# The down projection of a hybrid decoder layer by seven block products in place of eight

## The chip, the cores and the metric

The kernel runs on one core of one Trainium2 chip. The metric is the device time of one execution in microseconds (us). Below, PE is TensorE (matmul), PEld its weight load, DVE is VectorE, ACT is ScalarE, POOL is GpSimd and SP is SyncE, on which most DMA transfers are issued; ACT issues the others.

## The reference

One decoder layer on 512 tokens of 1024 channels: a mixer (matrix-memory heads beside a convolution group) and then a ConvFFN, each between two normalisations and with a residual. The change is in the ConvFFN's last part:

```python
u = rms_norm(x, ffn_pre_g[l]) * (1.0 + sc2) + sh2
up = causal_dwconv(u @ ffn_up[l], ffn_conv_w[l], ffn_conv_b[l])   # 1024 -> 2 x 2816, 3 taps
a, gt = jnp.split(up, 2, axis=-1)
f = (jax.nn.silu(gt) * a) @ ffn_down[l]                           # 512 x 2816 times 2816 x 1024
x = x + g2 * rms_norm(f, ffn_post_g[l])
```

## The kernel before

**Products.** Operands are float32. Each is split into a high part (rounded to the matmul's fp32r format) and a low part (the rest); a product of two operands is three matmuls, high by high, high by low and low by high (`mm3`, lines 186 to 190), all added into one PSUM bank. A matmul has a stationary block of 128 x 128 and a moving one of 128 x 512.

**Splitting weights.** `w_load` loads a row block of 128 x 2048 into one of two `raw` buffers from SP's queue; `w_split` makes the high part of each quarter on ACT (line 170) and the low part on POOL (line 171), into the pool `w` of 20 buffers.

**Up projection.** The loop over i = 0 to 21 (line 920 on) makes block i of `a` and of the gate on PE, does the three-tap convolution (ACT line 915, DVE line 917), the silu (ACT) and the product (DVE line 945), and splits the result into `fh` and `fl` (lines 951, 952), which lie with the contraction on the partitions and the 512 tokens along the row. They are kept in the pool of 44 `slot` buffers. `u2h` and `u2l` are the input's parts, in the pool `upool`.

**Down projection.** The result is four token tiles (tt) of 128 by two column halves (hf) of 512, one PSUM bank each: eight banks, all there are. For each of the 22 row blocks k of the weights every bank takes one `mm3`, tokens of `fh`/`fl` stationary and 512 weight columns moving: 22 x 4 x 2 x 3 = 528 matmuls. The first 18 row blocks go over all token tiles; the last four are done token tile after token tile (line 979), 24 matmuls each.

**The end.** For each token tile SP loads two residual tiles `xr` (line 985); DVE multiplies each bank by the gain row `g2r` (line 988), ACT takes the sum of squares, DVE and POOL make the token's factor (lines 615, 617), DVE adds the residual (line 993), and SP stores the result (line 994).

**Order.** PE and SP run their instructions in the order of the program text. On DVE, ACT and POOL a scheduler orders them when the program is built. Every engine then works its list strictly from the top, and each instruction waits there for what it needs: data, a buffer, or a transfer.

Of the kernel before, what the change touches and what calls it, by code (L numbers as in the profile page):

```python
# [14 lines left out]
ALU = mybir.AluOpType  # L15
# [37 lines left out]
def decoder_layer(ctx, tc, w_glu0, x, c, adaT, vecs, w_glu, w_qko, w_v0, w_v, w_out, w_up, w_down, out):  # L53
# [30 lines left out]
    def slot(name, dt=F32):  # L84
        return slots.tile([P, T], dt, tag="t", name=name)
# [4 lines left out]
    def atbank(name):  # L90
        return psum.tile([P, T], F32, tag="at", bufs=2, name=name)
# [528 lines left out]
    def tok(tt):  # L620
        return slice(tt * P, (tt + 1) * P)
# [298 lines left out]
    f = []  # L920
    for i in range(NF):
# [23 lines left out]
        V.tensor_tensor(out=a, in0=a, in1=g, op=ALU.mult)  # L945
# [5 lines left out]
        S.activation(hi, a, AF.Copy)  # L951
        V.tensor_tensor(out=lo, in0=a, in1=hi.bitcast(F32), op=ALU.subtract)
        f.append((hi, lo))


    KD = 18
    fsq = const.tile([P, 2 * NT], F32, name="fsq")
    banks = [[atbank(f"dn{tt}_{hf}") if tt == 0 else cvbank(f"dn{tt}_{hf}") if tt == 1 else mmbank(f"dn{tt}_{hf}")
              for hf in range(2)] for tt in range(NT)]
    wd = {}  # L960

    def down_rows(k):

        if k % 2 == 0:
            pieces = w_load(w_down[k // 2], f"wd{k}")
            wd[k], wd[k + 1] = pieces[:2], pieces[2:]
        return wd[k]

    def down_mm(k, tt):
        for hf in range(2):  # L970
            mm3(banks[tt][hf], (f[k][0][:, tok(tt)], f[k][1][:, tok(tt)]), wd[k][hf], k == 0, k == NF - 1)

    for k in range(KD):
        down_rows(k)
        for tt in range(NT):
            down_mm(k, tt)
    for k in range(KD, NF):
        down_rows(k)
    for tt in range(NT):
        for k in range(KD, NF):  # L980
            down_mm(k, tt)
# [4 lines left out]
        for hf in range(2):  # L986
            m = slot(f"fo{tt}_{hf}")
            V.tensor_tensor(out=m, in0=banks[tt][hf], in1=g2r[hf], op=ALU.mult)  # L988
            sq_sum(banks[tt][hf], fsq[:, 2 * tt + hf : 2 * tt + hf + 1], f"dn{tt}_{hf}")
            res.append(m)  # L990
# [6 lines left out]
def _layout(i):  # L997
# [9 lines left out]
    def tiles(w, starts, per):  # L1007
# [34 lines left out]
        "w_down": c_(f("ffn_down")[0].reshape(NF // 2, 2, P, D).transpose(0, 2, 1, 3).reshape(NF // 2, P, 2 * D)),  # L1042
# [19 lines left out]
```

## Time and profile before

| | us |
|---|---|
| median of 3 runs (797.0 to 800.23) | 797.66 |
| span of the profiled execution, first to last instruction | 794.8 |
| up projection's last matmul starts | 667.59 |
| down projection's first and last matmul start | 667.83, 787.44 |
| last store is issued (the second of two from 791.06) | 791.7 |

The page does not give the profiled execution's own time, only its span. A view of windows gives for each engine the busy time in a stretch, then the clock that TensorE was granted (1.00 is full), the share of the 16 DMA engines and the rate in GB/s. A row of the timeline has the start, the time, the engine, the line and what it writes and reads; "x2" joins two instructions in a row, so that the time shown for both is less than twice the mean where the second starts before the first has ended. In brackets is the engine's idle time before it and what ended that. The last number of a DMA row is the time from issue to landing.

### The profile page before, as it was taken

Reading aid. Unit: us, or ns where it says so; the run is one execution under the profiler, and the core shown is the slowest. Engines: PE = TensorE matmul, PEld = TensorE weight load, DVE = VectorE, ACT = ScalarE, POOL = GpSimd, SP = SyncE. Lnnn points to the kernel's source line nnn. Section 1 sums busy time; section 2 is a strip of 40 time slices with the busy share of each in tenths; the row PEclk is TensorE's granted clock in tenths of the full one; section 3 lists DMA queues with packets and bytes.
Section 4 is the critical chain, followed back from the end, with each engine's and each line's share of the span. In section 5 each row is a group of like instructions: output and inputs, shape, how many; then the busy total and the mean of one; then the engine's idle time right before and its main releaser. Section 6 shows DMA issues by size and latency. Waiting matters only on the chain.

```text
span 794.8 us, 10281 instructions
## 1 busy us (share of the span) xinstructions
PE 776.3 (98%) x3749; PEld 647.8 (81%) x3749; DVE 470.1 (59%) x737; ACT 378.5 (48%) x707; POOL 436.3 (55%) x357
## 2 busy tenths in 40 slices
PE   7899999899999999999999999999999999999996
PEld 4678898678888888888889988888888888888885
DVE  7659999999997334537968794454444453000014
ACT  6576428668574555561345454444444444222212
POOL 3689749769788443442941474444454444454420
PEclk9999999999999999999999999999999999999998
DMA  8973313313126331426854653322332222323205
GB/s 294 328 290 110 108 54 106 132 33 131 52 92 216 117 133 54 160 106 233 323 186 159 215 183 106 107 71 89 106 107 106 100 93 99 106 107 106 79 1 185
DMA packets 24886, 106.95 MB, mean 135 GB/s; under 512 B 2914, under 2 KB 2946, under 8 KB 17412
## 3 DMA queue, kind: packets, MB, share of 16 engines
q1 hardware_dynamic: 16740, 83.22, 29.9%
q10 hardware_dynamic: 8096, 23.08, 8.3%
q8 instruction: 29, 0.48, 0.3%
q14 instruction: 21, 0.17, 0.1%
HBM read 102.08 MB, written 4.21 MB: 134 GB/s over the span
## 4 chain that ended last, share of the span: by engine, by line
PE 73%; DVE 15%; DMA 4%; ACT 3%; issue 2%; POOL 1%; DVEq 0%; POOLq 0%; SPq 0%; ACTq 0%
PE up L189 10%; PE up L190 10%; PE up L188 10%; DVE cv L661 7%; PE dn L190 5%; PE dn L189 5%; PE dn L188 5%; PE glu L189 2%; PE glu L190 2%; PE glu L188 2%; DMA wglu<-in_w_glu 2%; PE mixa L190 2%; PE mixa L188 2%; PE mixa L189 2%; PE mixb L190 2%; PE mixb L189 2%
## 5 line engine op out<-in xcount | busy, mean ns | idle before, releaser
L661 DVE SCALAR_TENSOR_TENSOR cv<-gt,cvw,cv 128x506 f32<-128x506 f32 (+24 forms) x200 | 134.2, 728 | 0.4
L988 DVE TENSOR_TENSOR fo<-dn,g2r 128x512 f32<-128x512 f32 x8 | 5.5, 692 | 100.1 <-PE dn L190 100.1
L171 POOL TENSOR_TENSOR wup_1024l<-wup,wup_1024h 128x512 fp32r<-128x512 f32 x20 | 26.9, 1345 | 31.9 <-ACT wup_1024h L170 22.4
L171 POOL TENSOR_TENSOR wup_1536l<-wup,wup_1536h 128x512 fp32r<-128x512 f32 x20 | 27.1, 1355 | 29.1 <-ACT wup_1536h L170 29.0
L657 POOL TENSOR_TENSOR cs<-cs,cs 128x510 f32<-128x510 f32 (+3 forms) x32 | 41.8, 1305 | 0.2
L171 POOL TENSOR_TENSOR wup_512l<-wup,wup_512h 128x512 fp32r<-128x512 f32 x20 | 26.8, 1338 | 23.1 <-ACT wup_512h L170 23.1
L171 POOL TENSOR_TENSOR wup_0l<-wup,wup_0h 128x512 fp32r<-128x512 f32 x20 | 27.0, 1349 | 21.1 <-ACT wup_0h L170 21.1
L189 PE MATMUL up<-u2l,wup_0h 128*128 128x512 f32 (+1 forms) x100 | 36.5, 365 | 0.2 <-DVE u2l L830 0.2
L188 PE MATMUL up<-u2h,wup_0h 128*128 128x512 f32 (+1 forms) x100 | 36.5, 365 | 0.0
L188 PE MATMUL up<-u2h,wup_1024h 128*128 128x512 f32 (+1 forms) x100 | 36.5, 365 | 0.0
L190 PE MATMUL up<-u2h,wup_0l 128*128 128x512 f32 (+1 forms) x100 | 36.4, 364 | 0.0
L188 PE MATMUL up<-u2h,wup_1536h 128*128 128x512 f32 (+1 forms) x100 | 36.4, 364 | 0.0
L189 PE MATMUL up<-u2l,wup_1536h 128*128 128x512 f32 (+1 forms) x100 | 36.4, 364 | 0.0
L188 PE MATMUL up<-u2h,wup_512h 128*128 128x512 f32 (+1 forms) x100 | 36.4, 364 | 0.0
L190 PE MATMUL up<-u2h,wup_1536l 128*128 128x512 f32 (+1 forms) x100 | 36.4, 364 | 0.0
L189 PE MATMUL up<-u2l,wup_512h 128*128 128x512 f32 (+1 forms) x100 | 36.4, 364 | 0.0
L190 PE MATMUL up<-u2h,wup_512l 128*128 128x512 f32 (+1 forms) x100 | 36.4, 364 | 0.0
L190 PE MATMUL up<-u2h,wup_1024l 128*128 128x512 f32 (+1 forms) x100 | 36.4, 364 | 0.0
L189 PE MATMUL up<-u2l,wup_1024h 128*128 128x512 f32 (+1 forms) x100 | 36.4, 364 | 0.0
L155 DVE SCALAR_TENSOR_TENSOR junk<-ada,cb 128x1024 bf16<-128x1024 f32 x20 | 31.5, 1576 | 6.2 <-DMA ada<-in_adaT 6.0
L171 POOL TENSOR_TENSOR wd_1024l<-wd,wd_1024h 128x512 fp32r<-128x512 f32 x11 | 14.2, 1293 | 29.4 <-ACT wd_1024h L170 29.4
L171 POOL TENSOR_TENSOR wd_0l<-wd,wd_0h 128x512 fp32r<-128x512 f32 x11 | 14.3, 1296 | 28.0 <-ACT wd_0h L170 28.0
(723 smaller groups left out, 2613.5 us busy)
## 6 DMA issues: line engine op xcount, KB each, us to landing
wup<-in_w_up SPq DMA_DIRECT2D x22, 1024.0 KB, 4.8
wqko<-in_w_qko SPq DMA_DIRECT2D x12, 1024.0 KB, 4.8
wd<-in_w_down SPq DMA_DIRECT2D x11, 1024.0 KB, 4.8
ada<-in_adaT ACTq DMA_DIRECT2D x20, 512.0 KB, 5.6
ada<-in_adaT SPq DMA_DIRECT2D x16, 512.0 KB, 6.7
wo<-in_w_out SPq DMA_DIRECT2D x8, 1024.0 KB, 4.8
spare<-in_adaT ACTq DMA_DIRECT2D x12, 512.0 KB, 8.3
wglu<-in_w_glu SPq DMA_DIRECT2D x5, 1024.0 KB, 7.8
```

Source lines behind the costliest of these rows:

```text
L155: t = V.scalar_tensor_tensor(out=junk, in0=r, scalar=1.0, in1=cb, op0=ALU.mult, op1=ALU.mult, accum_out=mod[:, i : i + 1])
L171: (eng or G).tensor_tensor(out=lo[:, :n], in0=src, in1=hi[:, :n].bitcast(F32), op=ALU.subtract)
L188: PE.matmul(ps, a[0], b[0], start=start, stop=False)
L189: PE.matmul(ps, a[0], b[1], start=False, stop=False)
L190: PE.matmul(ps, a[1], b[0], start=False, stop=stop)
L657: G.tensor_tensor(out=side[:, d:], in0=side[:, d:], in1=t[:, d:], op=ALU.add)
L661: last_tap = V.scalar_tensor_tensor(out=cp[:, d:], in0=cvx[j][:, : T - d], scalar=w(CK - 1 - d), in1=cp[:, d:], op0=ALU.mult, op1=ALU.add)
L988: V.tensor_tensor(out=m, in0=banks[tt][hf], in1=g2r[hf], op=ALU.mult)
```

## The change

The contraction of 2816 is taken as eleven row blocks m of 2 x 128. In each, the activations are a 2 x 2 block matrix (two halves of 256 tokens by two halves of the contraction: a11, a12, a21, a22), and the weights too (b11 to b22, 128 x 512 each). Strassen's scheme in Winograd's form needs seven products of such blocks in place of eight. A product of one block is two token tiles q of 128, each with a bank of its own: 7 x 11 x 2 x 3 = 462 matmuls of the same shape.

Since seven products of two banks are 14 and there are eight banks, there are two phases. Phase one makes p1, p5, p6 and p7 over all m; phase two p2, p3 and p4. Between them the four sums are taken out of PSUM and added.

- In the up projection `forms` makes the combinations s1 to s4 of a pair of blocks on DVE (256 columns each), splits a11, s3, s1 and s2, and stores a12, a22 and s4 to DRAM (`g2_d`) from ACT's queue.
- In phase one `load1` loads three quarters of a weight row block, and `forms1` makes t1, t2 and t3 by three subtractions on DVE and splits four pieces. The high parts are ACT's as before, the low parts DVE's (function `split`); POOL has no part in it. t2 is stored to DRAM. There are two more raw buffers (`more`, in the place of `u2h`).
- In phase two `load2` loads two quarters and t2, `forms2` makes t4 and splits three pieces, `load_g2` loads the stored activations and `forms_g2` splits them.
- The end takes the token tiles in the order p2 and p3 for tiles 0 and 1, then p4 alone for tiles 2 and 3, whose other halves are complete after phase one. The last two row blocks (m = 9, 10) are done product after product in both phases.

The low parts of a weight row block of 2 x 128 before, on POOL (wd8 is the raw block, h and l are high and low parts; the last row is the next block's first):

```order
L171 TENSOR_TENSOR wd8_0l_6404<-wd8_6401,wd8_0h_6403 128x512
L171 TENSOR_TENSOR wd8_512l_6408<-wd8_6401,wd8_512h_6407 128x512
L171 TENSOR_TENSOR wd8_1024l_6412<-wd8_6401,wd8_1024h_6411 128x512
L171 TENSOR_TENSOR wd8_1536l_6416<-wd8_6401,wd8_1536h_6415 128x512
L171 TENSOR_TENSOR wd10_0l_6470<-wd10_6467,wd10_0h_6469 128x512
```

The same place now, on DVE in phase one (b, t and wd name weights; L1012 to L1014 are the subtractions, L927 the low parts):

```order
L1013 TENSOR_TENSOR wd1_5_6358<-wd1_5_6358 128x512
L927 TENSOR_TENSOR t2_4l_6447<-wd1_4_6311,t2_4h_6446 128x512
L927 TENSOR_TENSOR b1_5l_6481<-wd1_5_6358,b1_5h_6480 128x512
L1012 TENSOR_TENSOR wdmore_6238<-wdmore_6238 128x512
L1014 TENSOR_TENSOR wd1_5_6358<-wd1_5_6358 128x512
L927 TENSOR_TENSOR t1_5l_6485<-wd1_5_6358,t1_5h_6484 128x512
L927 TENSOR_TENSOR t3_5l_6489<-wd1_5_6358,t3_5h_6488 128x512
```

Four operations of POOL for each row block became seven of DVE; the subtractions of the next row block stand among the low parts of this one.

At the change of phase, on ACT, now (nothing corresponds to it before): g2h0 is the high part of the first stored activations, s40 that of their s4; t4_2h and b2_3h are weights of row blocks 2 and 3.

```order
L926 ACTIVATE t4_2h_6889<-wd2_13_6705 128x512
L926 ACTIVATE b2_3h_6924<-wdmore_6238 128x512
L926 ACTIVATE g2h0_6789<-g2kept_6239 128x512
L926 ACTIVATE s40_6791<-g2kept_6239 128x256
L926 ACTIVATE g2h1_6831<-g2kept_6239 128x512
```

And on DVE, where g2l0 is the low part, and su, s3 and sp5 are sums out of PSUM:

```order
L927 TENSOR_TENSOR t4_2l_6890<-wd2_13_6705,t4_2h_6889 128x512
L1085 TENSOR_TENSOR s3_0_6769<-p7_0_6236,su_0_6753 128x512
L1085 TENSOR_TENSOR s3_1_6770<-p7_1_6237,su_1_6754 128x512
L927 TENSOR_TENSOR b2_3l_6925<-wdmore_6238,b2_3h_6924 128x512
L1087 TENSOR_TENSOR su_0_6753<-su_0_6753,sp5_0_6737 128x512
L927 TENSOR_TENSOR g2l0_6790<-g2kept_6239,g2h0_6789 128x512
L1087 TENSOR_TENSOR su_1_6754<-su_1_6754,sp5_1_6738 128x512
L927 TENSOR_TENSOR s40_6791<-g2kept_6239,s40_6791 128x256
```

The first activations of phase two are split behind weights of its second and third row block, though the text asks for them first.

At the end on DVE, before: L988 is the product with g2r, L993 the residual addition.

```order
L988 TENSOR_TENSOR fo2_0_6883<-dn2_0_6133,g2r_5897 128x512
L988 TENSOR_TENSOR fo2_1_6887<-dn2_1_6134,g2r_5897 128x512
L615 TENSOR_SCALAR ro2t_6891<-fsq_6128 128x1
L993 SCALAR_TENSOR_TENSOR fo2_0_6883<-fo2_0_6883,ro2r_6893,xr2_0_6879 128x512
L993 SCALAR_TENSOR_TENSOR fo2_1_6887<-fo2_1_6887,ro2r_6893,xr2_1_6881 128x512
```

At the end on DVE, now: L1127 is the addition out of PSUM, L1130 the product with g2r, L1134 the residual addition.

```order
L1127 TENSOR_TENSOR su_1_6754<-p3_1_6780,su_1_6754 128x512
L1134 SCALAR_TENSOR_TENSOR fo0_0_7224<-fo0_0_7224,ro0r_7233,xr0_0_7217 128x512
L1134 SCALAR_TENSOR_TENSOR fo0_1_7229<-fo0_1_7229,ro0r_7233,xr0_1_7219 128x512
L1130 TENSOR_TENSOR fo1_1_7263<-su_1_6754,g2r_5981 128x512
L1127 TENSOR_TENSOR s3_0_6769<-p4_0_6781,s3_0_6769 128x512
L615 TENSOR_SCALAR ro1t_7265<-fsq_6229 128x1
L1127 TENSOR_TENSOR s3_1_6770<-p4_1_6782,s3_1_6770 128x512
L1130 TENSOR_TENSOR fo2_0_7286<-s3_0_6769,g2r_5981 128x512
L615 TENSOR_SCALAR ro2t_7288<-fsq_6229 128x1
L1130 TENSOR_TENSOR fo3_0_7309<-s3_1_6770,g2r_5981 128x512
L615 TENSOR_SCALAR ro3t_7311<-fsq_6229 128x1
L1134 SCALAR_TENSOR_TENSOR fo1_0_7258<-fo1_0_7258,ro1r_7267,xr1_0_7251 128x512
```

Before, the operations of one token tile stand together; now the second tile's residual additions stand behind the sums of tiles two and three. SP's order is the same as before: the two stores of a tile, then the two xr of the next.

The diff, cut:

```diff
--- before.py
+++ after.py
@@ -917,7 +917,33 @@
             V.scalar_tensor_tensor(out=t[:, d:], in0=ps[:, : T - d], scalar=w(2 - d), in1=t[:, d:], op0=ALU.mult, op1=ALU.add)
         return t
 
-    f = []
+    NM = NF // 2
+    g2_d = [dram.tile([P, 3 * HT], F32, tag=f"g2d{m}", name=f"g2d{m}") for m in range(NM)]
+    t2_d = [dram.tile([P, T], F32, tag=f"t2d{m}", name=f"t2d{m}") for m in range(NM)]
+    pairs = []
+
+    def split(src, hi, lo):
+        S.activation(hi, src, AF.Copy)
+        V.tensor_tensor(out=lo, in0=src, in1=hi.bitcast(F32), op=ALU.subtract)
+
+    def forms(m, F):
+
+        a11, a21, a12, a22 = (F[:, b * HT : (b + 1) * HT] for b in range(4))
+        s1, s2 = ysum[:, :HT], ysum[:, HT:]
+        s4 = ysq[:, (m % 2) * HT : (m % 2 + 1) * HT]
+        V.tensor_tensor(out=s1, in0=a21, in1=a22, op=ALU.add)
+        V.tensor_tensor(out=a21, in0=a11, in1=a21, op=ALU.subtract)
+        V.tensor_tensor(out=s2, in0=s1, in1=a11, op=ALU.subtract)
+        V.tensor_tensor(out=s4, in0=a12, in1=s2, op=ALU.subtract)
+        own = []
+        for n, z in enumerate((F[:, :T], ysum)):
+            hi, lo = slot(f"fh{m}_{n}", F32R), slot(f"fl{m}_{n}", F32R)
+            split(z, hi, lo)
+            own.append((hi, lo))
+        pairs.append(own)
+        nc.scalar.dma_start(g2_d[m][:, :T], F[:, T : 2 * T])
+        nc.scalar.dma_start(g2_d[m][:, T:], s4)
+
     for i in range(NF):
...
         a = conv3(pa, i, f"fa{i}")
         g = conv3(pg, NF + i, f"fg{i}")
         S.activation(g, g, AF.Silu)
-        V.tensor_tensor(out=a, in0=a, in1=g, op=ALU.mult)
-        if i < 2:
-            hl = vpool.tile([P, 2 * T + 8], F32R, tag="vh", name=f"fhl{i}")
-            hi, lo = hl[:, :T], hl[:, T : 2 * T]
+        if i % 2 == 0:
+            F = vpool.tile([P, 2 * T + 8], F32, tag="vh", name=f"F{i // 2}")
+        V.tensor_tensor(out=F[:, (i % 2) * T : (i % 2 + 1) * T], in0=a, in1=g, op=ALU.mult)
+        if i % 2:
+            forms(i // 2, F)
+
+
+    M1 = NM - 2
+    M2 = NM - 2
+    fsq = const.tile([P, 2 * NT], F32, name="fsq")
+    p1 = [atbank(f"p1_{q}") for q in range(2)]
+    p5 = [cvbank(f"p5_{q}") for q in range(2)]
+    p6 = [mmbank(f"p6_{q}") for q in range(2)]
+    p7 = [mmbank(f"p7_{q}") for q in range(2)]
+    more = upool.tile([P, 2, 2048], F32, tag="uh", name="wdmore")
+    kept = upool.tile([P, 5, 3 * HT], F32, tag="ul", name="g2kept")
+
+    def wd_raw(m, n):
+        return raws.tile([P, 2048], F32, tag="raw", name=f"wd{n}_{m}") if m % 4 < 2 else more[:, m % 2, :]
+
+    def parts(r, names):
+        out = {}
+        for name, b in names:
+            hi, lo = wpool.tile([P, T], F32R, tag="w", name=f"{name}h"), wpool.tile([P, T], F32R, tag="w", name=f"{name}l")
+            split(r[:, b * T : (b + 1) * T], hi, lo)
+            out[name[:2]] = (hi, lo)
+        return out
+
...
+    loaded = {}
+
+    def load1(m):
+        loaded[m] = r = wd_raw(m, 1)
+        nc.sync.dma_start(r[:, T:], w_down[m][:, T:])
+
+    def forms1(m):
+
+        r = loaded.pop(m)
+        t3, b11, b12, b22 = (quarter(r, b) for b in range(4))
+        V.tensor_tensor(out=t3, in0=b22, in1=b12, op=ALU.subtract)
+        V.tensor_tensor(out=b12, in0=b12, in1=b11, op=ALU.subtract)
+        V.tensor_tensor(out=b22, in0=b22, in1=b12, op=ALU.subtract)
+        w = parts(r, [(f"b1_{m}", 1), (f"t1_{m}", 2), (f"t3_{m}", 0), (f"t2_{m}", 3)])
+        nc.sync.dma_start(t2_d[m], b22)
+        return w
+
+    def load2(m):
+        loaded[m] = r = wd_raw(m + NM, 2)
+        nc.sync.dma_start(r[:, :T], w_down[m][:, :T])
+        nc.sync.dma_start(r[:, T : 2 * T], w_down[m][:, 3 * T :])
+        nc.sync.dma_start(r[:, 2 * T : 3 * T], t2_d[m])
+
+    def forms2(m):
+
+        r = loaded.pop(m)
+        V.tensor_tensor(out=quarter(r, 2), in0=quarter(r, 0), in1=quarter(r, 2), op=ALU.subtract)
+        return parts(r, [(f"b2_{m}", 0), (f"b4_{m}", 1), (f"t4_{m}", 2)])
+
+    def load_g2(m):
+        nc.sync.dma_start(kept[:, m % 5, :], g2_d[m])
+
+    def forms_g2(m):
+        r = kept[:, m % 5, :]
+        h, l, s = slot(f"g2h{m}", F32R), slot(f"g2l{m}", F32R), slot(f"s4{m}", F32R)
+        split(r[:, :T], h, l)
+        split(r[:, T:], s[:, :HT], s[:, HT:])
+        return [(h[:, :HT], l[:, :HT]), (h[:, HT:], l[:, HT:]), (s[:, :HT], s[:, HT:])]
+
...
+    def prod1(m, which):
+        (a11, s3), (s1, s2) = (halves_of(z) for z in pairs[m])
+        ps, form, w = {"p1": (p1, a11, "b1"), "p5": (p5, s1, "t1"), "p7": (p7, s3, "t3"), "p6": (p6, s2, "t2")}[which]
+        for q in range(2):
+            mm3(ps[q], part(form, q), w1[m][w], m == 0, m == NM - 1)
+
+    w1, w2, g2 = {}, {}, {}
+    for m in range(3):
+        load1(m)
+    for m in range(NM):
+        w1[m] = forms1(m)
+        if m + 3 < NM:
+            load1(m + 3)
         else:
-            hi, lo = slot(f"fh{i}", F32R), slot(f"fl{i}", F32R)
-        S.activation(hi, a, AF.Copy)
-        V.tensor_tensor(out=lo, in0=a, in1=hi.bitcast(F32), op=ALU.subtract)
-        f.append((hi, lo))
-
-
-    KD = 18
-    fsq = const.tile([P, 2 * NT], F32, name="fsq")
-    banks = [[atbank(f"dn{tt}_{hf}") if tt == 0 else cvbank(f"dn{tt}_{hf}") if tt == 1 else mmbank(f"dn{tt}_{hf}")
-              for hf in range(2)] for tt in range(NT)]
-    wd = {}
-
-    def down_rows(k):
-
-        if k % 2 == 0:
-            pieces = w_load(w_down[k // 2], f"wd{k}")
-            wd[k], wd[k + 1] = pieces[:2], pieces[2:]
-        return wd[k]
-
-    def down_mm(k, tt):
-        for hf in range(2):
-            mm3(banks[tt][hf], (f[k][0][:, tok(tt)], f[k][1][:, tok(tt)]), wd[k][hf], k == 0, k == NF - 1)
-
-    for k in range(KD):
-        down_rows(k)
-        for tt in range(NT):
-            down_mm(k, tt)
-    for k in range(KD, NF):
-        down_rows(k)
+            load2(m + 3 - NM)
+        if m < 5:
+            load_g2(m)
+        if m < M1:
+            for which in ("p1", "p5", "p7", "p6"):
+                prod1(m, which)
+    for which in ("p1", "p5", "p6", "p7"):
+        for m in range(M1, NM):
+            prod1(m, which)
...
+        elif which == "p6":
+            su = [slot(f"su_{q}") for q in range(2)]
+            for q in range(2):
+                V.tensor_tensor(out=su[q], in0=p6[q], in1=sp1[q], op=ALU.add)
+        else:
+            s3 = [slot(f"s3_{q}") for q in range(2)]
+            for q in range(2):
+                V.tensor_tensor(out=s3[q], in0=p7[q], in1=su[q], op=ALU.add)
+    for q in range(2):
+        V.tensor_tensor(out=su[q], in0=su[q], in1=sp5[q], op=ALU.add)
+        V.tensor_tensor(out=sp5[q], in0=sp5[q], in1=s3[q], op=ALU.add)
+    p2 = [atbank(f"p2_{q}") for q in range(2)]
+    p3 = [cvbank(f"p3_{q}") for q in range(2)]
+    p4 = [mmbank(f"p4_{q}") for q in range(2)]
+
+    def prod2(m, which, q):
+        a12, a22, s4 = g2[m]
+        ps, form, w = {"p2": (p2, a12, "b2"), "p3": (p3, s4, "b4"), "p4": (p4, a22, "t4")}[which]
+        mm3(ps[q], part(form, q), w2[m][w], m == 0, m == NM - 1)
+
+    for q in range(2):
+        sq_sum(sp5[q], fsq[:, 2 * (2 + q) + 1 : 2 * (2 + q) + 2], f"c22_{q}")
+    for q in range(2):
+        V.tensor_tensor(out=sp5[q], in0=sp5[q], in1=g2r[1], op=ALU.mult)
+    for m in range(NM):
+        g2[m] = forms_g2(m)
+        w2[m] = forms2(m)
+        if m + 3 < NM:
+            load2(m + 3)
+        if m + 5 < NM:
+            load_g2(m + 5)
+        if m < M2:
+            for which in ("p2", "p3", "p4"):
+                for q in range(2):
+                    prod2(m, which, q)
     for tt in range(NT):
-        for k in range(KD, NF):
-            down_mm(k, tt)
+        q = tt % 2
+        for which in ("p2", "p3") if tt < 2 else ("p4",):
+            for m in range(M2, NM):
+                prod2(m, which, q)
         res, xr = [], []
         for hf in range(2):
             xr.append(cvtile(f"xr{tt}_{hf}"))
             nc.sync.dma_start(xr[hf], x1_d[tt][hf])
-        for hf in range(2):
+        for hf, pair in enumerate(((p2[q], sp1[q]), (p3[q], su[q])) if tt < 2 else ((p4[q], s3[q]), None)):
+            if pair is None:
+                res.append(sp5[q])
+                continue
+            ps, z = pair
+            V.tensor_tensor(out=z, in0=ps, in1=z, op=ALU.add)
+            sq_sum(z, fsq[:, 2 * tt + hf : 2 * tt + hf + 1], f"dn{tt}_{hf}")
             m = slot(f"fo{tt}_{hf}")
-            V.tensor_tensor(out=m, in0=banks[tt][hf], in1=g2r[hf], op=ALU.mult)
-            sq_sum(banks[tt][hf], fsq[:, 2 * tt + hf : 2 * tt + hf + 1], f"dn{tt}_{hf}")
+            V.tensor_tensor(out=m, in0=z, in1=g2r[hf], op=ALU.mult)
             res.append(m)
...
```

More of the change, by code (lines that the diff above doesn't have):

```diff
@@ new lines, in quarter @@
+    def quarter(r, b):
+        return r[:, b * T : (b + 1) * T]
+    loaded = {}
[11 more added lines that the diff above has]
+        return w
@@ new lines, in forms_g2, with part, halves_of @@
+    def forms_g2(m):
[4 more added lines that the diff above has]
+        return [(h[:, :HT], l[:, :HT]), (h[:, HT:], l[:, HT:]), (s[:, :HT], s[:, HT:])]
+    def part(form, q):
+        return tuple(z[:, q * P : (q + 1) * P] for z in form)
+    def halves_of(pair):
+        return [tuple(z[:, h * HT : (h + 1) * HT] for z in pair) for h in range(2)]
```

11 lines of the change are left out of this document (10 added, 1 removed).

## The prediction

> **What bounds the kernel now.** I read the page first, then the windows over the down projection, then the timeline of its first and last microseconds.
>
> ```profile
> PE 776.3 (98%) x3749; PEld 647.8 (81%) x3749; DVE 470.1 (59%) x737; ACT 378.5 (48%) x707; POOL 436.3 (55%) x357
> PE 73%; DVE 15%; DMA 4%; ACT 3%; issue 2%; POOL 1%; DVEq 0%; POOLq 0%; SPq 0%; ACTq 0%
> DVE  7659999999997334537968794454444453000014
> 668.00:741.00 73.00, 73.00 (x323) 60.30 (x323) 2.88 (x4) 18.66 (x30) 34.09 (x27) 1.00 0.26 92
> 667.83 0.39 PE L188 MATMUL dn<-wd_0h,fhl 128*128 128x512 f32 x1
> 787.44 0.39 PE L190 MATMUL dn<-wd_1536h,fl 128*128 128x512 f32 x1
> ```
>
> TensorE (PE) is busy throughout. The window of the down projection (columns: PE, weight load, DVE, ACT, POOL, clock, DMA share, GB/s) shows it full at clock 1.00 while VectorE (DVE) does next to nothing and the DMA engines are used to 26%. The stage is therefore TensorE's. Its 528 products start at 667.83 and the last starts at 787.44: 119.61 us over 527 steps, 0.227 us each. I call 667.83 t = 0.
>
> What follows the last product is the other part that sets the end:
>
> ```profile
> 787.19 1.37 DVE L988 TENSOR_TENSOR fo<-dn,g2r 128x512 f32<-128x512 f32 x2 [0.93 <-PE dn L190]
> 789.71 0.54 POOL L617 TENSOR_TENSOR ro3r<-ro3t,mhalf 128x1 f32<-128x1 f32 x1 [4.90 <-DVE ro3t L615]
> 790.28 1.42 DVE L993 SCALAR_TENSOR_TENSOR fo<-fo,ro3r,xr 128x512 f32<-128x512 f32 x2 [0.66 <-POOL ro3r L617]
> 791.06 1.00 SPq L994 DMA_DIRECT2D out<-fo  x2
> 780.18 1.00 SPq L994 DMA_DIRECT2D out<-fo  x2
> 781.24 0.95 SPq L985 DMA_DIRECT2D xr<-x1d  x2
> xr<-x1d SPq DMA_DIRECT2D x8, 256.0 KB, 3.2
> out<-fo SPq DMA_DIRECT2D x8, 256.0 KB, 2.0
> L994 SPq DMA_DIRECT2D out<-fo x8: 337/338/338, 774.7 to 791.7; - x8
> ```
>
> The last product ends at E = 787.83. The last two residual additions end 3.9 us later (790.28 + 1.42), and the span ends at 794.8, E + 7.0. SyncE (SP) issues a token tile's two residual loads (xr) only after the stores of the tile before, and such a load lands 3.2 us after its issue. Now that costs nothing: the four tiles finish 24 products, 5.4 us, apart.
>
> **The change, part by part.**
>
> *Products.* 7 x 11 x 2 x 3 = 462 in place of 528, of the same shape: 66 x 0.227 = **-15.0 us**. TensorE's order is 66 rows shorter, so the saving is real in the program.
>
> *Phase one on VectorE.* The low parts of the weights move from GpSimd (POOL) to VectorE, with three subtractions: 7 operations of 128x512 for each row block, against 24 products, 5.45 us.
>
> ```profile
> 437.03 0.68 DVE L171 TENSOR_TENSOR wup_1024l<-wup,wup_1024h 128x512 fp32r<-128x512 f32 x1
> 437.63 1.28 DVE L830 TENSOR_TENSOR u2l<-xT,u2h 128x512 fp32r<-128x512 f32 x2
> 438.83 0.70 DVE L171 TENSOR_TENSOR wup_1536l<-wup,wup_1536h 128x512 fp32r<-128x512 f32 x1
> 437.48 0.63 ACT L170 ACTIVATE wup_512h<-wup 128x512 fp32r<-128x512 f32 x1
> 438.00 0.62 ACT L170 ACTIVATE wup_1024h<-wup 128x512 fp32r<-128x512 f32 x1
> 672.20 0.63 ACT L951 ACTIVATE fh<-fa21c 128x512 fp32r<-128x512 f32 x1 [0.76 <-DVE fa21c L945]
> wd<-in_w_down SPq DMA_DIRECT2D x11, 1024.0 KB, 4.8
> wv<-in_w_v SPq DMA_DIRECT2D x6, 512.0 KB, 3.3
> ```
>
> One such operation lasts 0.69 but the next starts 0.60 after it (437.03, 437.63, 438.83); ScalarE (ACT) starts one each 0.52. Seven cost 4.3 us at 0.61, 4.8 at 0.69: below 5.45. The first two row blocks are split while the up projection still runs, on an idle VectorE. The third load waits for the last product of the up projection, since it takes the place of u2h; 768 KB lie halfway between 3.3 and 4.8, so it lands near t = 4.3, just when VectorE has finished the last gate (672.20). Its weights are needed from t = 10.9 on, and up to there VectorE does 15 operations, 9 us: it is ahead. Cost 0; without that lead (0.69 and nothing overlapped) it shows at the phase change, below.
>
> *The phase change.* Phase one ends at P = 264 x 0.227 = 59.9. Nothing of the second half of the activations is split before: g2h0 stands behind b2_3h on ScalarE, whose slot the very last p7 product frees, and g2l0 behind five operations on VectorE, the first of which (t4_2l) needs a slot that the p7 products of row block 9 free at P - 1.4. ScalarE makes t4_2h by P - 0.75; from there VectorE runs t4_2l, s3_0, s3_1, b2_3l, su_0 at 0.60 and g2l0 at 0.69: ready at P + 3.0. ScalarE's own part is ready at P + 0.52 + 0.63 = 1.2, so two of the first three products run meanwhile (0.45) and TensorE loses **+2.6 us**. Lower end: 1.2, ScalarE's part alone. Upper end: VectorE has 85 wide and 4 half-wide operations from t = 4.3 to g2l0; at 0.69 without overlap these are 60.1, with 0.6 for a load it waits for, 65.0: P + 5.1, a loss of 4.6. I take 2.6, since the rows with this operation show 0.60.
>
> A rule on such a hole was weighed here.
>
> ```profile
> 789.90:790.40 0.50, 0.00 (x0) 0.00 (x0) 0.12 (x1) 0.00 (x0) 0.35 (x1) 1.00 0.00 0
> 790.40:790.90 0.50, 0.00 (x0) 0.00 (x0) 0.50 (x1) 0.00 (x0) 0.00 (x0) 0.51 0.00 0
> ```
>
> After the last product the granted clock falls from 1.00 to 0.51 some 2.6 us on. The hole at the phase change comes in pieces of 1.0 and 1.5 us with products between, shorter than that, so I add nothing. The Trainium skill ("TensorE: Matmul & The Clock Gate", The HAM clock gate) says that an idle window of about 3.4 us halves the clock, and that it takes another such busy window to return. By it alone, a hole that did catch a window would cost about 1.7 us more, an estimate from that figure.
>
> *Phase two.* 18 products for each row block, 4.09 us, against 5 wide operations and a half on VectorE (3.4 at 0.61, 3.8 at 0.69). Loads: 768 KB of weights and differences and 384 KB of activations for each, 1.18 MB in 4.09 us, 288 GB/s.
>
> ```profile
> 432.00:436.00 4.00, 4.00 (x36) 4.00 (x35) 3.69 (x7) 2.91 (x8) 0.54 (x1) 1.00 0.97 362
> 775.70:779.50 3.80, 3.80 (x18) 3.15 (x17) 1.68 (x4) 1.38 (x4) 0.54 (x1) 1.00 0.85 262
> ```
>
> The engines moved 362 GB/s in one stretch, and with pieces of 2 KB a row 262 at 85%, 308 at full use. So 0; upper end +3, if 262 were all (10% of 33 us). Phase one asks 264 GB/s and starts ahead.
>
> *Up projection.* Four half-wide operations and two stores more in each pair of blocks, 21.8 us. VectorE is 40 to 50% busy there (its row of the 40 slices, the stretch of 4s and 5s) and TensorE's weights are split ahead of it: 0. If ScalarE's wait for the stores ate that lead, a microsecond.
>
> *The end.* A token tile now follows the one before by 12, then 6 and 6 products: 2.7, 1.4 and 1.4 us in place of 5.4. Each of the first two takes two additions out of PSUM, two products with g2r and two residual additions on VectorE, so VectorE falls behind. At E - 2.7 (p3_1 complete) its order still holds, up to the second tile's last residual addition: three additions, three products, four residual additions and three short ones. The ten wide ones, at 0.60 to 0.67 where the next is independent and 0.73 where it waits for the one before, are 6.6; with the short ones and the last one's full length, it is done at E + 4.4. The first tile's stores go out at E - 0.3, so the second's xr are there by E + 3.4: no wait yet. Then the SyncE order bites: store 0.34, xr of tile three issued at E + 4.8, landed at E + 8.0, two residual additions (0.67 + 0.75) to E + 9.45; store, xr of tile four at E + 9.85, landed at 13.05, additions to E + 14.5. Before, that point was E + 3.9: **+10.6 us**. Lower end: the two loads come in 2.0 as the stores do, 2 x 1.2 less, +8.2. Upper end: no overlap on VectorE, 1.2 more, +11.8. I take 10.6, since all eight xr took 3.1 to 3.2.
>
> **Sum.** -15.0 + 2.6 + 10.6 = -1.8. The profiled span of 794.8 becomes 793.0. The page does not give that execution's own time; the median of the runs shown, 797.66, is 2.9 above the span, and I keep these 2.9 around it: 795.9, rounded **796 us**. The ends of the terms give -15.0 + 1.2 + 8.2 = -5.6 (792.1) and -15.0 + 4.6 + 11.8 + 3 = +4.4 (802.1).
>
> **The rivals.**
>
> *VectorE becomes the bound (slower).* Its low parts wait for ScalarE's high parts, and these for freed slots. If each of its 85 operations up to g2l0 cost a handshake, 0.79 in place of 0.61, it would get there at t = 4.9 + 67.2 + 1.6 = 73.7, and TensorE would lose 13.3 us in phase one or at its end: -15.0 + 13.3 + 10.6 = +8.9, 806.6. It begins to decide at 0.67 each, and passes half a per cent near 0.73. For it: the row of 672.20 and its like show VectorE and ScalarE waiting for each other 0.7 us at a time where each needs the other's last result. Against it: in the changed order a high part is asked for two or three operations ahead, and the rows of 437 to 439 have the same operation with the same partner at 0.60.
>
> *The end is cheaper (faster).* If the two residual loads land in 2.0, and TensorE waits only for ScalarE at the phase change, the time is 792.1. For it: nothing else loads in these microseconds. Against it: in the old end nothing else loaded either, and the loads took 3.2.
>
> *The DMA engines decide phase two.* 262 GB/s would add 3: 799. For it: 2 KB rows and three times the bytes of before. Against it: three row blocks of lead, and 85% use in that row.
>
> That the program does not save its products is excluded by the order.
>
> **How the numbers follow.** Forecast near 796: 0.45. DMA-bound phase two: 0.10. VectorE bound: 0.28. Cheaper end: 0.17. What can be told from no change here is about 0.5%, 4 us: 793.7 to 801.7. The forecast and the DMA case lie inside, the VectorE case above, the cheaper end below: faster 0.17, same 0.55, slower 0.28. For 8 in 10 the range takes the lower ends whole, 792, and reaches from 802.1 into the VectorE case, to 804.
>
> **What would show it.** The first and last product of the down projection about 107.2 us apart (461 x 0.227 + 2.6); one hole of 2 to 3 us on TensorE at the change from p7 to p2, ended by VectorE's g2l0, and none at p1 of the third block; xr loads of tiles three and four each followed by VectorE idling about 3 us; the span's end about 17.6 us after the last product in place of 7.0. Holes ended by VectorE's low parts within phase one would make the second rival right; an end of less than 14 us, the cheaper one.

## The result, and the profile after

The change makes no difference that can be measured: 797.51 us (median of 20 runs) against 797.75 before (20 runs), ratio 0.9989 with a 95% interval of 0.9974 to 1.0005. The profiled execution took 795.99 us, 1.7 more than its span of 794.3.

The page of the changed kernel, its busy line and the chain of work that ended last:

```profile
PE 763.7 (96%) x3683; PEld 636.6 (80%) x3683; DVE 591.8 (75%) x938; ACT 408.3 (51%) x766; POOL 384.0 (48%) x313
PE 72%; DVE 15%; DMA 6%; ACT 3%; issue 2%; POOL 1%; SPq 0%; DVEq 0%; POOLq 0%; ACTq 0%
```

66 matmuls are gone and VectorE works 122 us more, yet PE's share of the chain hardly moves: of what left PE, part became waits for DMA (4% to 6%). Where the time went is read from three places. First the change of phase (timeline; the last p7, then p2; g2h and g2l are the split activations):

```profile
728.70 0.39 PE L190 MATMUL p<-t_10h,fl 128*128 128x512 f32 x1
728.89 0.63 ACT L926 ACTIVATE b_3h<-wdmore 128x512 fp32r<-128x512 f32 x1 [0.72 <-PE p L189]
729.43 0.61 ACT L926 ACTIVATE g2h<-g2kept 128x512 fp32r<-128x512 f32 x1
730.10 0.50 PE L188 MATMUL p<-b_0h,g2h 128*128 128x512 f32 x1 [1.01 <-ACT g2h L926]
730.43 0.40 PE L189 MATMUL p<-b_0l,g2h 128*128 128x512 f32 x1
730.45 0.69 DVE L927 TENSOR_TENSOR b_3l<-wdmore,b_3h 128x512 fp32r<-128x512 f32 x1
731.05 0.69 DVE L1087 TENSOR_TENSOR su<-su,sp 128x512 f32<-128x512 f32 x1
731.65 0.69 DVE L927 TENSOR_TENSOR g2l<-g2kept,g2h 128x512 fp32r<-128x512 f32 x1
732.40 0.50 PE L190 MATMUL p<-b_0h,g2l 128*128 128x512 f32 x1 [1.57 <-DVE g2l L927]
```

VectorE works without a break; it comes to g2l only after weights of row block 3 and a sum. From the second product behind g2l on, the pace is 0.23 again.

Then the end (SPq rows are issues on SP's queue):

```profile
776.73 0.39 PE L190 MATMUL p<-t_10h,g2l 128*128 128x512 f32 x1
...
780.84 1.00 SPq L1135 DMA_DIRECT2D out<-fo  x2
781.88 0.94 SPq L1121 DMA_DIRECT2D xr<-x1d  x2
784.84 0.75 DVE L1134 SCALAR_TENSOR_TENSOR fo<-fo,ro2r,xr 128x512 f32<-128x512 f32 x1 [3.37 <-DMA xr<-x1d]
785.51 0.74 DVE L1134 SCALAR_TENSOR_TENSOR sp<-sp,ro2r,xr 128x512 f32<-128x512 f32 x1
785.62 0.34 SPq L1135 DMA_DIRECT2D out<-fo  x1
786.28 0.34 SPq L1135 DMA_DIRECT2D out<-sp  x1
786.67 0.95 SPq L1121 DMA_DIRECT2D xr<-x1d  x2
789.90 0.75 DVE L1134 SCALAR_TENSOR_TENSOR fo<-fo,ro3r,xr 128x512 f32<-128x512 f32 x1 [3.65 <-DMA xr<-x1d]
790.57 0.75 DVE L1134 SCALAR_TENSOR_TENSOR sp<-sp,ro3r,xr 128x512 f32<-128x512 f32 x1
```

The last product ends at E = 777.12. Twice VectorE stands still over 3 us for a load whose issue stands behind the stores of the tile before. The last addition ends at E + 14.2 (before: E + 3.9), the span at E + 17.2 (before: E + 7.0).

Third, a stretch far ahead of the change, in the mixer, from the windows view (the number before the last two is the granted clock); first the kernel before, then the changed one:

```profile
150.00:160.00 10.00, 7.61 (x38) 6.34 (x38) 9.94 (x17) 7.52 (x15) 6.34 (x6) 1.00 0.16 52
```

```profile
150.00:160.00 10.00, 7.63 (x30) 6.24 (x31) 9.94 (x17) 7.52 (x16) 6.56 (x6) 0.83 0.16 52
...
733.00:760.00 27.00, 27.00 (x121) 22.35 (x120) 26.55 (x49) 18.97 (x39) 0.00 (x0) 1.00 0.90 312
```

In the changed kernel's profiled execution the clock fell for some 3.4 us there, in that of the kernel before it did not, and the first down product starts at 669.08 in place of 667.83. This belongs to the execution and not to the change: two of the runs below that are the kernel before up to this point show the fall too (0.83 in the same window in e5_before_xr_first, 0.66 in e4_before_less_66), and in the runs below the first down product starts anywhere from 668.03 to 670.25.

The balance of the two spans: start +1.25, products -15.0, change of phase +3.0 (the first and the last product are 107.65 us apart, 461 steps of 0.227 are 104.65), end +10.2. The sum is -0.55; measured 794.8 to 794.3. Against the run below that has no hole at the change of phase (104.5) the change of phase is 3.2.

### The profile page after: what moved, and what is told of

The parts are those of the page before. It is cut to its first block, busy times and chain, and to the rows that moved or that the text cites. A ratio compares the mean times of both kernels' runs of the same rounds, so it can differ in the third digit from the quotient of the medians.

```text
span 794.3 us, 10575 instructions
## 1 busy us (share of the span) xinstructions
PE 763.7 (96%) x3683; PEld 636.6 (80%) x3683; DVE 591.8 (75%) x938; ACT 408.3 (51%) x766; POOL 384.0 (48%) x313
## 4 chain that ended last, share of the span: by engine, by line
PE 72%; DVE 15%; DMA 6%; ACT 3%; issue 2%; POOL 1%; SPq 0%; DVEq 0%; POOLq 0%; ACTq 0%
PE up L190 10%; PE up L189 10%; PE up L188 10%; DVE cv L661 5%; PE p L190 3%; PE p L188 3%; PE p L189 3%; PE glu L189 3%; PE glu L190 3%; PE glu L188 3%; PE qko L189 2%; PE qko L188 2%; PE qko L190 2%; PE mixa L190 2%; PE mixa L188 2%; PE mixa L189 2%
## 5 line engine op out<-in xcount | busy, mean ns | idle before, releaser
L655 ACT ACTIVATE cs<-gt,cvw 128x511 f32<-128x511 f32 (+4 forms) x40 | 27.2, 711 | 4.4 <-POOL cs L657 3.7
L171 POOL TENSOR_TENSOR wqko_1024l<-wqko,wqko_1024h 128x512 fp32r<-128x512 f32 x12 | 16.6, 1380 | 22.4 <-PE v L189 12.3
```

The costliest lines, as they stand in the source:

```text
L171: (eng or G).tensor_tensor(out=lo[:, :n], in0=src, in1=hi[:, :n].bitcast(F32), op=ALU.subtract)
L655: S.activation(t[:, d:], cvx[j][:, : T - d], AF.Copy, scale=w(CK - 1 - d))
```

## The experiments

"First to last" is from the start of the first down product to that of the last, "end" from the end of the last product to the end of the span, both from the profiled execution. Ratios are to the kernel before on the same chip. The runs with a letter and a number are medians of 4 to 12 executions.

| run | median us | ratio, 95% interval | span | first to last | end |
|---|---|---|---|---|---|
| kernel before | 797.75 | 1 | 794.8 | 119.6 | 7.0 |
| changed kernel | 797.51 | 0.9989 (0.9974 to 1.0005) | 794.3 | 107.65 | 17.2 |
| e1_xr_first | 789.04 | 0.9889 (0.9873 to 0.9906) | 786.8 | 107.2 | 10.2 |
| e2_g2_before_tail | 793.72 | 0.9937 (0.9924 to 0.9949) | 790.8 | 104.5 | 16.8 |
| e3_both | 787.25 | 0.9854 (0.9839 to 0.9868) | 785.2 | 106.05 | 9.7 |
| e4_before_less_66 | 783.39 | 0.9809 (0.9794 to 0.9823) | 782.3 | 104.65 | 7.0 |
| e5_before_xr_first | 798.41 | 1.0009 (0.9993 to 1.0026) | 795.7 | 119.6 | 7.0 |
| d1_one_more_op | 801.39 | 1.0037 (1.0018 to 1.0056) | 799.3 | 111.8 | 17.0 |
| d2_two_more_ops | 811.61 | 1.0171 (1.0143 to 1.0199) | 810.4 | 122.1 | 19.4 |
| f1_two_blocks_early | 786.55 | 0.9851 (0.9834 to 0.9867) | 784.3 | 104.5 | 9.7 |
| f3_p4_first_pool | 787.54 | 0.9862 (0.9843 to 0.9881) | 784.3 | 104.5 | 11.0 |
| e6_no_gain_row | 783.11 | 0.9813 (0.9787 to 0.9839) | 781.0 | 104.5 | 8.1 |

**The end alone.** The eight residual tiles get the place of the spare raw buffer `more`, and are loaded ahead of the loop over the token tiles.

```diff
+    xrs = [[more[:, tt // 2, ((tt % 2) * 2 + hf) * T : ((tt % 2) * 2 + hf + 1) * T] for hf in range(2)] for tt in range(NT)]
+    for tt in range(NT):
+        for hf in range(2):
+            nc.sync.dma_start(xrs[tt][hf], x1_d[tt][hf])
     for tt in range(NT):
...
-            xr.append(cvtile(f"xr{tt}_{hf}"))
-            nc.sync.dma_start(xr[hf], x1_d[tt][hf])
```

> The eight residual tiles go into the raw buffer that phase two no longer needs and are all issued ahead of the tail, so no load stands behind a store; the rest is the changed kernel. Theory (the end is lengthened by the two loads of 3.2 us that each wait for stores of the tile before): VectorE no longer idles before the residual additions of tiles three and four; the last one ends near 6.8 us after the last product in place of 14.2, the span falls by 7.4 us, to about 787 (time 790, ratio to before 0.991). Rival (the end is long because VectorE, ScalarE and GpSimd have that much work and hand-overs behind the last product; the loads are only seen waiting): the waits turn into others and no more than 2 us are gained (796, ratio 0.996 or more).

The theory holds. VectorE's last operations in this run's timeline, behind a last product that ends at 776.65:

```profile
780.59 0.75 DVE L1135 SCALAR_TENSOR_TENSOR fo<-fo,ro2r,wdmore 128x512 f32<-128x512 f32 x1
781.25 0.75 DVE L1135 SCALAR_TENSOR_TENSOR sp<-sp,ro2r,wdmore 128x512 f32<-128x512 f32 x1
782.43 0.75 DVE L1135 SCALAR_TENSOR_TENSOR fo<-fo,ro3r,wdmore 128x512 f32<-128x512 f32 x1 [0.44 <-POOL ro3r L617]
783.10 0.75 DVE L1135 SCALAR_TENSOR_TENSOR sp<-sp,ro3r,wdmore 128x512 f32<-128x512 f32 x1
```

No wait for a load is left, and the last addition ends at E + 7.2. The end is 7.0 us shorter, the span 7.5; the other half microsecond is a shorter hole at the change of phase (107.2 from first to last), where the two programs have the same order, so this hole seems to vary by as much from one execution to the next.

**The same edit in the kernel before,** with a free buffer in the place of `u2h`:

> The kernel before, with its eight residual loads issued ahead of the tail into a free buffer. Theory (there the tiles end 5.4 us apart and the loads of 3.2 us are hidden; the wait for them is made by the closer tiles of the change): no difference, ratio 0.998 to 1.002. Rival (the loads cost something in the old end too, so that part of the gain of the same edit in the changed kernel has nothing to do with the change): 1 to 3 us less, ratio 0.996 to 0.999 with an interval that leaves out 1.

No difference: the end stays at 7.0, and the interval holds 1. The order of SP's queue cost nothing there; the closer tiles of the change made it cost 7.

**The change of phase alone.** The call that splits the first stored activations is moved up in the text, ahead of the products that end phase one. I read the old order so: their buffers come from a pool that gives them out in the order of the text, so they had to follow those of the sums. The run shows that the place in the text decides, but not by which rule.

```diff
+    g2[0] = forms_g2(0)
     for which in ("p1", "p5", "p6", "p7"):
         for m in range(M1, NM):
...
     for m in range(NM):
-        g2[m] = forms_g2(m)
+        if m >= 1:
+            g2[m] = forms_g2(m)
```

> The split of the first stored activations (g2h0, g2l0 and the part of s4) stands ahead of the tail of phase one in the text, so that it is asked for and gets its buffers before the sums out of PSUM; the rest is the changed kernel. Theory (the hole at the phase change is a matter of order: g2h0 behind b2_3h, g2l0 behind three sums and b2_3l): the hole of 3.0 us at the change from p7 to p2 goes to less than 0.3, the span falls by 3 us to about 791.3 (ratio to before 0.995). Rival (VectorE is out of time at the phase change, and whatever it does first something else is late): the hole reappears within the next two row blocks, before p4 of the first or p2 of the second, and less than 1 us is gained.

The hole is gone, as these rows of TensorE show at the same place (0.23 from the last p7 on):

```profile
728.69 0.39 PE L190 MATMUL p<-t_10h,fl 128*128 128x512 f32 x1
728.92 0.39 PE L188 MATMUL p<-b_0h,g2h 128*128 128x512 f32 x1
729.15 0.39 PE L189 MATMUL p<-b_0l,g2h 128*128 128x512 f32 x1
729.37 0.39 PE L190 MATMUL p<-b_0h,g2l 128*128 128x512 f32 x1
```

g2l is now made at 683.39 in place of 731.65. First to last is 104.5, the span is 3.5 shorter, and nothing is late behind it. The hole was a matter of order.

**Both together:**

> The residual loads first and the split ahead of the tail of phase one, together. Theory (the two costs lie in different places and add up): the span falls by 10.4 us to about 784 (time 787, ratio to before 0.987), faster than both kernels. Rival (one of the two hides the other, the end being set by something that runs through): the gain is that of the larger alone, 7.4 us, ratio 0.991.

9.1 us of the span in place of 10.4; the kernel is faster than both. The missing part is a hole at the second row block:

```profile
733.56 0.68 DVE L1088 TENSOR_TENSOR su<-su,sp 128x512 f32<-128x512 f32 x1
734.16 0.69 DVE L927 TENSOR_TENSOR g2l<-g2kept,g2h 128x512 fp32r<-128x512 f32 x1
```

```profile
734.90 0.50 PE L190 MATMUL p<-b_1h,g2l 128*128 128x512 f32 x1 [1.26 <-DVE g2l L927]
```

The second row block's activations now stand behind the sums. They did so in the run before too, without a hole; here VectorE gets there 1.85 us later than there (732.31), after a wait of 1.40 for a load of t2 that was 0.17 there:

```profile
725.84 0.69 DVE L1028 TENSOR_TENSOR wdmore<-wdmore 128x512 f32<-128x512 f32 x1 [1.40 <-DMA wdmore<-t2d]
```

So this order leaves no room for a late load; how often one is late is not shown. Next, two row blocks are split early:

```diff
+    g2[0] = forms_g2(0)
+    g2[1] = forms_g2(1)
```

> The residual loads first, and the activations of the first two row blocks of phase two split ahead of the tail of phase one, in place of the first alone. Theory (with the first split early, the second became the one that stands behind the sums: a hole of 1.3 us before its first product with a low part): no hole is left between the phases, first to last product 104.7 us, span about 784 (time 785.8, ratio to before 0.984). Rival (VectorE is short of time there, and the hole moves on to the third row block): the span stays at 785.

First to last is 104.5 and the trace shows no wait on TensorE in the down projection. The time, 0.9851, cannot be told from the 0.9854 of the run with one row block early.

**What the products are worth.** In the kernel before, 66 products are left out and nothing else is touched.

```diff
+            if 1 <= k <= 8 or (k == 9 and tt == 0):
+                x, w = (f[k][0][:, tok(tt)], f[k][1][:, tok(tt)]), wd[k][hf]
+                PE.matmul(banks[tt][hf], x[0], w[0], start=False, stop=False)
+                PE.matmul(banks[tt][hf], x[0], w[1], start=False, stop=False)
+                continue
             mm3(
```

> The kernel before with 66 of its 528 down products left out (the product of the activations' low part with the weights' high part in row blocks 1 to 8, and for one token tile in row block 9), so that it does not compute the reference; nothing else is changed. Theory (a product is worth 0.227 us and nothing else bounds the stage): first to last product 104.6 us, span 15.0 us less, about 779.8, ratio to before 0.981: what the change would bring without its by-costs. Rival (the splitting of the weights, at 5.5 us of GpSimd for two row blocks, or their loads then set the pace in the thinned blocks): 3 to 6 us of the 15 stay, ratio 0.985 to 0.989.

First to last falls by 15.0 (119.6 to 104.65), and the ratio of 0.9809 is 15.2 us. So the saving is whole, and the change gave all but a fraction of it back.

**How near VectorE is to its limit.** One or two idle operations in each weight row block:

```diff
+        for _ in range(1):
+            V.tensor_tensor(out=extra, in0=b12, in1=b11, op=ALU.add)
         w = parts(r, [(f"b1_{m}", 1), (f"t1_{m}", 2), (f"t3_{m}", 0), (f"t2_{m}", 3)])
...
+        for _ in range(1):
+            V.tensor_tensor(out=extra, in0=quarter(r, 0), in1=quarter(r, 1), op=ALU.add)
         return parts(r, [(f"b2_{m}", 0), (f"b4_{m}", 1), (f"t4_{m}", 2)])
```

> The changed kernel with one idle VectorE operation of 128x512 more in each weight row block of both phases (its result is used by nothing). Theory (VectorE stays below TensorE's pace of 5.45 us for a row block, but what it does in phase one adds up to the phase change, where only the 4.4 us that it idled after 678 are free): no hole within phase one; some 14 operations of 0.60 come ahead of g2l0, 8.4 us, and the hole at the phase change grows from 3.0 by 4 us to about 7; span about 798, time 801.5, ratio to before 1.004. Rival (only the pace within a row block counts, and 8 x 0.60 = 4.8 us are below it): less than 1 us is lost. Second rival (each operation costs a handshake with ScalarE, so that VectorE is at its limit already): holes at the first product of a row block within phase one, more than 8 us lost.

> The same with two idle operations more in each weight row block. Theory: 9 x 0.60 = 5.4 us, still just below 5.45 in phase one; some 28 operations, 16.8 us, come ahead of g2l0, 4.4 of them free: the hole at the phase change grows by 12.4 us to about 15, time 810, ratio 1.015. Rival (pace only): less than 2 us lost. Second rival (VectorE at its limit): 16 us or more, in holes spread over phase one.

One more costs 4.2 us between first and last product, as forecast, and nothing inside phase one; but the sum is made in another way. From 9.2 us after the first down product on (678.3 in the changed kernel, 679.3 here) VectorE has 93 operations up to g2l in place of 82 (twelve extra ones; those of the first three row blocks were done before, and one sum moved behind g2l): 6.6 us, of which 4.4 fill its idle time. g2l is 2.2 us later than in the changed kernel (P + 5.6 against P + 3.4, P being where phase one ends), and the clock, which fell in this hole, added the rest:

```profile
731.08 0.50 PE L188 MATMUL p<-b_0h,g2h 128*128 128x512 f32 x1 [1.01 <-ACT g2h L926]
735.58 0.79 PE L190 MATMUL p<-b_0h,g2l 128*128 128x512 f32 x1 [3.76 <-DVE g2l L927]
...
736.17 0.63 PE L188 MATMUL p<-b_0h,g2h 128*128 128x512 f32 x1
736.60 0.63 PE L189 MATMUL p<-b_0l,g2h 128*128 128x512 f32 x1
...
739.58 0.51 PE L190 MATMUL p<-b_0h,s 128*128 128x512 f32 x1
739.93 0.40 PE L188 MATMUL p<-t_0h,g2h 128*128 128x512 f32 x1
```

Some ten products come at 0.43 in place of 0.227, 2.0 us. Two more cost 14.4 us in place of 12.4, but not where they were forecast: 2.0 are lost within phase one, 5.0 more than in the changed kernel at the change of phase, and 7.4 from there on, nearly all near the end of phase two. That the sum came out near is partly luck. Who TensorE waited for in that run (sum, times, longest):

```profile
PE p L190 <- DVE g2l L927: 4.7, 1, 4.7
PE p L188 <- ACT b_10h L926: 4.0, 1, 4.0
PE p L189 <- DVE t_10l L927: 1.7, 1, 1.7
```

At nine operations VectorE is late within phase one too (t_10l) and at the change of phase; near the end of phase two ScalarE's b_10h stands behind a load that comes late. After the two longest of these waits the products again come at 0.43 for a while. So the rival by which only the pace within a row block counts falls, and the one by which VectorE was at its limit in the changed kernel falls as well: eight operations a row block make no hole in phase one.

**What is left at the end.** First another order of the tiles, with GpSimd doing four of the six products with the gain row:

```diff
-    for tt in range(NT):
+    for tt in (2, 3, 0, 1):
         q = tt % 2
...
-            V.tensor_tensor(out=m, in0=z, in1=g2r[hf], op=ALU.mult)
+            (V if tt == 1 else G).tensor_tensor(out=m, in0=z, in1=g2r[hf], op=ALU.mult)
```

> As the kernel with two row blocks early, and at the end the order of token tiles is changed: p4 of tiles three and four first, then p2 and p3 of tile one, then of tile two; the products with the gain row go to GpSimd, but for the tile that ends last. Theory (with the loads out of the way, VectorE's 20 wide operations from the first finished product on set the end: 13 us from 6.8 us before the last product): four or five fewer of them bring the last residual addition from 7.2 to about 6 us after the last product, span about 783 (time 784.7, ratio 0.983). Rival (the factors that GpSimd makes now stand behind its own products of 1.4 us each): no gain or a loss of a microsecond.

The rival is right: the end is 11.0 in place of 9.7, the last addition at E + 8.0 (the times, 787.54 and 786.55, are too close to tell). VectorE's rows and then GpSimd's:

```profile
770.52 1.77 DVE L1138 SCALAR_TENSOR_TENSOR fo<-fo,ro2r,wdmore 128x512 f32<-128x512 f32 x1 [0.48 <-POOL ro2r L617]
772.21 0.74 DVE L1138 SCALAR_TENSOR_TENSOR sp<-sp,ro2r,wdmore 128x512 f32<-128x512 f32 x1
...
774.07 1.43 DVE L1138 SCALAR_TENSOR_TENSOR fo<-fo,ro3r,wdmore 128x512 f32<-128x512 f32 x1
775.43 0.74 DVE L1138 SCALAR_TENSOR_TENSOR sp<-sp,ro3r,wdmore 128x512 f32<-128x512 f32 x1
```

```profile
770.45 1.29 POOL L1134 TENSOR_TENSOR fo<-sp,g2r 128x512 f32<-128x512 f32 x1
771.70 0.99 POOL L617 TENSOR_TENSOR ro3r<-ro3t,mhalf 128x1 f32<-128x1 f32 x1
773.68 1.27 POOL L1134 TENSOR_TENSOR fo<-su,g2r 128x512 f32<-128x512 f32 x1 [0.99 <-issue]
```

Two of the factors (ro2r and ro3r) wait behind GpSimd's products, and VectorE's additions beside these take 1.77 and 1.43 us in place of 0.74. The order of the tiles was changed in the same run, so what each of the two edits costs is not shown. Then the products with the gain row are left out:

```diff
-            m = slot(f"fo{tt}_{hf}")
-            V.tensor_tensor(out=m, in0=z, in1=g2r[hf], op=ALU.mult)
-            res.append(m)
+            res.append(z)
```

> The kernel with the residual loads first and two row blocks early, but without the six products with the gain row g2r at the end (so that those parts of the output lack that factor). Theory (with the loads out of the way the end is set by VectorE's throughput: 20 wide operations of 0.60 to 0.67 from the first finished product on): six of 0.60 fewer, and the last residual addition moves from 6.7 us behind the last product to 3.5 at the latest, near the 3.9 of the kernel before; span about 781 (time 783, ratio 0.981). Rival (the chain from the last product on sets it: addition, sum of squares on ScalarE, factor on VectorE and GpSimd, residual additions): less than 1 us gained.

Between the two: the last addition ends at E + 5.1 (778.00, the last product at 772.91), 1.6 us earlier than with the products, not 3.2:

```profile
777.25 0.75 DVE L1136 SCALAR_TENSOR_TENSOR sp<-sp,ro3r,wdmore 128x512 f32<-128x512 f32 x1
```

VectorE then idles early in the tail, waiting for products, and has no break only from E + 0.9 on. Its work is part of the remaining 9.7 us, but not all of it; which tile order would be best stays open.

## Why the prediction was right

The forecast was 796 and no change; measured 797.51 and no change. The mechanism is as written: the products save 15 us, and the change of phase and the end take nearly all of it back. That the terms add up to the forecast -1.8 (-15.0 + 3.0 + 10.2) is partly luck, since one came out 0.4 above and one 0.4 below. Its steps:

- *Products, -15.0:* measured -15.0, both in the changed kernel and alone.
- *Phase one, 0:* no wait on TensorE there. VectorE's operations follow each other at 0.60 from 679 to 703 without a gap, the rate that was taken from the rows of 437 to 439; it finishes a row block in 4.2 us against 5.45, and idles 4.4 us between 703 and 724, 3.4 of them by the trace for loads. The third load landed at t = 5.1 (from the first down product), not 4.3, without effect.
- *Up projection, 0:* right. From its first product to its last it takes 243.4 us in both kernels (424.23 to 667.59 before, 425.49 to 668.86 now).
- *Change of phase, +2.6:* measured 3.0. The pattern is as written, two products between two waits, and so are releasers and order: g2h at P + 1.1 (forecast 1.2), g2l done at P + 3.4 (3.0). The term was 0.4 too small because I let VectorE begin t4_2l as soon as t4_2h was there, at P - 0.75; that was there in time (728.17), but VectorE, coming late from two sums, still had another low part to do (728.05) and began at P - 0.28.
- *Clock at the change, 0:* right in the number, but the reason given, that the pieces are too short, is not shown. In the changed kernel's profiled execution the clock is 1.00 from 727 to 733. In the run with one more operation it fell at P + 3.1, when its hole of 3.8 us was 1.2 us old. Up to that point TensorE's rows are the same in both kernels, and the changed kernel's hole was still open too (to P + 3.5). So the length of the hole did not decide alone, other executions of the changed kernel may have such a fall, and its absence here was partly luck. In that run it cost 2.0 us. By the Trainium skill's rule ("TensorE: Matmul & The Clock Gate", The HAM clock gate) the prediction had an estimate of 1.7. The two are near by chance: the clock was low for 6.8 us (733.0 to 739.8), not for 3.4, and the 3.4 us before the fall were not idle, since TensorE started three products in them (the last at 731.42).
- *Phase two, 0:* right. The stretch from 733 to 760 moved 312 GB/s at a DMA share of 0.90, more than the 288 worked out, and TensorE was full; the rival of the DMA engines falls.
- *The end, +10.6:* measured 10.2. The second tile's additions end at E + 4.35 (forecast 4.4), though after a wait of 0.24 us for their own load (780.06), where the forecast had none. The loads of tiles three and four are issued at E + 4.8 and E + 9.55 (4.8 and 9.85) and take 3.2 to 3.3 us. The cheaper end falls: beside the tile's own stores nothing else used the DMA engines, and the loads took as long as before.
- *VectorE as the bound:* falls, by the two runs with more operations. Eight operations a row block leave phase one without a hole; one more cost 4.2 us at the change of phase, as the sum over the whole phase has it.
- *The 2.9 us around the span:* this step was wrong. An execution takes 1.7 more than its span (795.99 against 794.3), so the profiled execution of the kernel before took some 796.5 and was one of its quicker ones. The span came out 1.3 above the forecast of 793.0, by the later start; the two errors cancel in the profiled execution (795.99), which is luck, and the median of the 20 lies 1.5 above that. No term of the change is in this.

The gain thus went into two places that the change opened and that do not belong to its arithmetic: a queue order at the end and an engine order in the middle. Undoing both leaves 0.985, with 2.7 us of a longer end, against 0.981 for the products alone.

## What to carry to other kernels

A change that removes work from the bounding engine also removes time that covered something else: ask at the end of each stage what was hidden only because results came far apart, and read SP's order of stores and loads there. Where an engine works through a list, the first operand of the next phase belongs ahead of the sums that close the last one; the price of such an order is counted in operations of the engine, and the repair costs no operation. The repaired kernel is faster than both, by 1.5% against the kernel before (0.9851, 0.9834 to 0.9867).

## What the runs showed of the hardware

- The granted clock falls to half for about 3.4 us in the mixer in most executions profiled here (0.83 in 150 to 160), for twice as long in two (0.66), and not at all in two (1.00). Among kernels that share everything up to the up projection the start of the down projection varied by 2.4 us (667.83 to 670.25), more than the whole effect of the change.
- Behind phase one the clock fell to half in the run with one more operation, whose holes there are 1.0 and 3.8 us, and not in the changed kernel, whose holes are 1.0 and 1.6. It fell 1.2 us into the longer hole, at a point up to which the two runs are alike. After the last product had ended it fell 2.0 us later in e2_g2_before_tail, 2.6 in the kernel before and 4.7 in the changed kernel. So a fall follows idle time, but how long a wait brings it cannot be read from its length alone. First the changed kernel, then the run with one more operation:

```profile
727.00:733.00 6.00, 3.42 (x15) 2.20 (x14) 6.00 (x11) 4.26 (x9) 0.00 (x0) 1.00 0.00 0
```

```profile
731.00:733.00 2.00, 0.73 (x2) 0.30 (x2) 2.00 (x4) 2.00 (x7) 0.00 (x0) 1.00 0.00 0
733.00:735.50 2.50, 0.00 (x0) 0.00 (x0) 2.50 (x6) 1.64 (x4) 0.00 (x0) 0.50 0.00 0
...
740.00:741.50 1.50, 1.50 (x8) 1.24 (x7) 1.50 (x4) 0.63 (x2) 0.00 (x0) 1.00 0.71 181
```

  The clock is the third number from the right.
- A residual addition of VectorE with two wide inputs in SBUF took 1.77 and 1.43 us beside a GpSimd product, 0.74 without one. The Trainium skill ("SBUF — State Buffer", SBUF: two separate sides) says that such an operation and a GpSimd operation that reads SBUF lock each other out; the rows agree with it, since both end 0.55 us after the GpSimd product beside them has ended (771.74 and 774.95).
